# A hybrid encoder step on one core: sample caches read in turned order, new keys and rows written unturned, sample keys in blocks of 96, 96 and 80

## The chip, the core and the metric

The kernel runs on one core of one Trainium2 chip. The metric is the device time of one execution in microseconds (us); the figure given is the median of several runs. The profile is of one execution, taken by the hardware profiler. Engines are TensorE (PE; its weight loads are PEld), VectorE (DVE), ScalarE (ACT), GpSimd (POOL) and SyncE (SP). L12 is line 12 of the kernel before.

## What is computed

One layer of a streaming encoder, in float32, for 2048 prompt tokens (16 tiles of 128) and for a sample group of 8 streams with 16 new tokens each (one more tile of 128). Model width is 1024. What matters here of the reference:

```python
proj = h @ w_in                                   # q | k | v | u_val | u_gate, 512 each
k_ext = jnp.concatenate([past_k, k], axis=1)      # per stream 256 cached keys, 16 new ones
att = band_attention(q, k_ext, v_ext, ...)        # 8 heads of 64
u = u_val * jax.nn.sigmoid(u_gate)
u_ext = jnp.concatenate([conv_buf, u], axis=1)    # 30 cached rows, then a causal conv of width 31
new_k, new_v, new_conv = k_ext[:, -keep:], v_ext[:, -keep:], u_ext[:, -30:]
x = x + rmsnorm(jnp.concatenate([att, c], -1) @ w_out, g_mix_post)
mk, mv = (rmsnorm(mem, g_mem) @ w).reshape(...)   # 256 memory tokens, prompt only
x = x + rmsnorm(memory_attention(rmsnorm(x), mk, mv, w_mq, w_mo), g_mem_post)   # 4 heads of 256
x = x + rmsnorm((silu(h @ w_gate) * (h @ w_up)) @ w_down, g_ffn_post)
```

Outputs are the two activations, the newest keys, values and convolution rows of both groups, and the memory keys and values of the prompt. For the sample group the 256 memory keys and values per stream come in as caches.

## The kernel before, in words

Every product is made with float32 operands split in two parts, `hi` and `lo`, the second being what the rounding of the first left over (`mm3`, L286: three matmuls for one product, at L288, L289, L290; `mm3h`, L292, the same in two halves of 512 columns, at L296). ScalarE writes `hi`, VectorE or GpSimd subtracts (`wload`, L274: load on the SyncE queue, L277; cast, L281; subtraction, L283). Small products of the sample group's attention are plain float32, which the trace shows as two TensorE instructions each.

A matmul contracts over partitions, so operands must stand with the contracted index on partitions. What arrives with tokens on partitions is turned by `nc.tensor.transpose`, a matmul against the identity (`ident`) into PSUM, and copied out by ScalarE.

The phases, in order:

- **Memory phase** (`phase_mem`, L371). For `w_mk`, then `w_mv`: eight blocks of 128 output columns. Each block loads a weight block, makes 24 matmuls, and VectorE copies the result, with columns on partitions, into `yf` (L428, three buffers); splits of it go to `yh` and `yl` for the products that follow. For the output, `transp` (L410) turns each block with two transposes (L413) and two copies (L415) into `ot`, which is stored as rows at the end (L437).
- **Projections** (`phase_proj`, L464). Three groups of six (the last: five) tiles. First `conv_halo` (L483) brings the 30 cached convolution rows of each stream into `us`: two loads, eight transposes (L489), eight scaled copies (L491). Per group come gate and value products, the values `vo`, and then keys and queries in `qk` (L697). For tiles of 12 and over, the last group, `qk` copies each key tile (L721), transposes it (L723) and gathers it in `ko` (L726), stored as rows (L730, L732). The new convolution rows are turned too (L684 to L696). `tick` and `pump` mix in the convolution, on VectorE and GpSimd, at a rate per step.
- **Attention** (`attention`, L768). 128 units of one head and one tile, written out as a pipeline: scores at unit i, transposes of the probabilities four units later (L891), values six later (L904). `sample(s)`, L791, is a generator that handles stream s beside head s; the loop takes one of its steps every second unit from the second head on. Its steps: loads of the cached keys `kc`, values `vc` and new values `vn`; two steps of four transposes (L805) each with a copy into `kt` (L806); GpSimd's copy of the 16 new keys into `kt` (L808); scores over 272 keys (L819) and softmax; three transposes of the probabilities (L828); the value products. These take the keys in blocks of 128, 128 and 16: for each of four column groups two products with 128 partitions (L837) and one with 16 (L838).
- **Output projection and the sample group's memory attention** (`mixout`, L1000; `cross_sample`, L1085). The prompt tiles' products (L296) are the main stream. `cross_sample` is a generator of which one step is taken for every two of the eight weight blocks of a tile: norm, query product, 16 half streams of keys, softmax, 16 half streams of values, output product. `keys` (L1177) loads two blocks of 128 memory tokens per stream, and for each half of the width makes eight transposes (L1186) with two casts (L1188) and two subtractions (L1189); `Ahead` makes it two jobs early. `vals` (L1226) needs no transpose: `load` (L1105), then `split` (L1098: cast L1101, subtraction L1102). Both use three load buffers `wf`.
- **Prompt memory attention, gate and up, down.** The change does not touch their arithmetic. `shift_caches` (L1388) copies the kept part of the key and value caches from DRAM to DRAM during gate and up.

Storage is laid out by hand: a `Region` gives each name a place, a size and a count of buffers in a few large arenas, and names of different phases share places. The order of instructions on each engine comes from the tile framework, which orders the program when it is built by a simulated timeline (L1725), with some priorities set by hand. On the chip every engine and the SyncE queue then works through its own list in that order.

Of the kernel before, what the change touches and what calls it, by code (L numbers as in the profile page):

```python
# [31 lines left out]
PAST = 256  # L32
EPS = 1e-6
# [105 lines left out]
class Build:  # L139
# [22 lines left out]
    def early(self, ctx):  # L162
# [10 lines left out]
                   .lay(sbF, 18, ("kxx", 0.5, 2), ("vo", 1, 3), ("ko", 2, 5))  # L173
# [5 lines left out]
                        ("ctmp", 3, 2), ("qh", 1.5, 2), ("ql", 1.5, 2), ("kx", 0.5, 2))  # L179
# [191 lines left out]
    def phase_mem(self):  # L371
# [4 lines left out]
                .lay(fa, 0, ("f2o", 8, 2), ("ot", 4, 2), ("ss", 0.03125, 6), ("rstd", 0.03125, 6))  # L376
# [26 lines left out]
        for which, wn, on in ((0, "w_mk", "new_mem_k_prompt"), (1, "w_mv", "new_mem_v_prompt")):  # L403
# [3 lines left out]
            ot = [self.t(pool, [P, D], F32, "ot", 2) for _ in range(2)]  # L407
            prev = None

            def transp(j, yf):  # L410
                pt = self.t(ps_tr, [P, 2, P], F32, "tr")
                for i in range(2):
                    nc.tensor.transpose(pt[:, i, :], yf[:, i * P:(i + 1) * P], self.ident[:, :])  # L413
                for i in range(2):
                    nc.scalar.copy(ot[i][:, j * P:(j + 1) * P], pt[:, i, :])  # L415

            for j in range(KC):
# [14 lines left out]
                if prev is not None:  # L432
                    transp(*prev)
                prev = (j, yf)
            transp(*prev)
            for i in range(2):
                nc.sync.dma_start(A[on][i * P:(i + 1) * P, :], ot[i][:, :])  # L437
# [26 lines left out]
    def phase_proj(self):  # L464
# [18 lines left out]
        def conv_halo():  # L483
            for i in range(2):
                cc = self.t(pool, [P, D], F32, "xt", 2)
                nc.sync.dma_start(cc[:120, :512], A["cache_conv"][i * 120:(i + 1) * 120, :])
                pt = self.t(ps_tr, [P, 4, P], F32, "tr")
                for j in range(4):
                    nc.tensor.transpose(pt[:, j, :120], cc[:120, j * P:(j + 1) * P], self.ident[:120, :120])  # L489
                for j in range(4):  # L490
                    nc.scalar.activation(us[:, j, 4 * i:4 * i + 4, :HALO],  # L491
                                         pt[:, j, :120].rearrange("p (s w) -> p s w", w=HALO), AF.Copy, scale=2.0)
# [101 lines left out]
        kos = {}  # L594
        nxt = [norm_sub(GROUPS[0][0]), norm_sub(GROUPS[0][1])]
        conv_halo()
        for gi, subs in enumerate(GROUPS):
# [52 lines left out]
            for cg in range(2):  # L650
                wv = [self.wload(A["w_v"][cg, kh]) for kh in range(2)]
                for hsub, sub in zip(hs, subs):
                    hh, hl, _, _ = hsub
                    for i, t in enumerate(sub):
# [7 lines left out]
                        if t >= 12:  # L662
                            vo = self.t(pool, [P, 256], F32, "vo")
                            nc.scalar.copy(vo[:, :], ps[:, :256])
                            if t == S_TILE:
                                nc.sync.dma_start(self.vsamp[:, cg * 256:(cg + 1) * 256], vo[:, :])
                                nc.sync.dma_start(
                                    A["new_att_v_sample"][:, PAST - DEC_S:, cg * 256:(cg + 1) * 256], vo[:, :])
# [12 lines left out]
            if last:  # L681
                pt = self.t(ps_tr, [P, 4, P], F32, "tr")
                for j in range(4):
                    nc.tensor.transpose(pt[:HALO, j, :], uts[j][:, L:L + HALO], self.ident[:, :])  # L684
                un = self.t(pool, [P, 4, P], F32, "xn", 2)
                nc.scalar.activation(un[:HALO], pt[:HALO, 0:4, :], AF.Copy, scale=0.5)
                nc.sync.dma_start(A["new_conv_prompt"], un[:HALO].rearrange("p a b -> p (a b)"))
                pt = self.t(ps_tr, [P, 4, P], F32, "tr")
                for j in range(4):
                    uc = self.t(pool, [P, P], F32, "kx" + x_, 2)  # L690
                    nc.gpsimd.tensor_copy(uc[:, :].rearrange("p (s w) -> p s w", w=DEC_S), us[:, j, :, HALO:])
                    nc.tensor.transpose(pt[:, j, :], uc[:, :], self.ident[:, :])
                un = self.t(pool, [P, 4, P], F32, "xn", 2)
                nc.scalar.activation(un[:, :, :], pt[:, 0:4, :], AF.Copy, scale=0.5)
                nc.sync.dma_start(A["new_conv_sample"][:, HALO - DEC_S:, :],
                                  un[:, :, :].rearrange("p a b -> p (a b)"))  # L696
            def qk(which, j, blk, x):  # L697
# [14 lines left out]
                else:  # L712
# [4 lines left out]
                    for i, t in enumerate(sub):  # L717
                        if t < 12:
                            continue
                        kx = self.t(pool, [P, P], F32, "kx" + x_, 2)  # L720
                        nc.scalar.copy(kx[:, :], ps[:, i * P:(i + 1) * P])  # L721
                        pt = self.t(ps_tr, [P, 4, P], F32, "tr")
                        nc.tensor.transpose(pt[:, 0, :], kx[:, :], self.ident[:, :])  # L723
                        if j == 0:
                            kos[t] = self.t(pool, [P, 512], F32, "ko")
                        nc.scalar.copy(kos[t][:, j * P:(j + 1) * P], pt[:, 0, :])  # L726
                        if j < 3:
                            continue
                        if t == S_TILE:
                            nc.sync.dma_start(A["new_att_k_sample"][:, PAST - DEC_S:, :], kos[t][:, :])  # L730
                        else:
                            nc.sync.dma_start(A["new_att_k_prompt"][(t - 12) * P:(t - 11) * P, :], kos[t][:, :])  # L732
# [32 lines left out]
        nc.sync.dma_start(A["new_conv_sample"][:, :HALO - DEC_S, :],  # L765
                          A["cache_conv"].rearrange("(s w) d -> s w d", w=HALO)[:, DEC_S:, :])

    def attention(self):  # L768
        nc, A = self.nc, self.A
        sbF, sbR, ps, fa, fb = self.sbF, self.sbR, self.ps, self.fa, self.fb  # L770
        pool = (Region().lay(sbF, 34.5, ("kc", 4, 2), ("kt", 4.25, 1), ("pp", 1.5, 1), ("vn", 2, 1))
                .at("z", 2.5, (fa, [25, 22.5, 15, 20, 17.5]), (fb, [0, 2.5, 5]))
                .lay(fb, 7.5, ("vc", 4, 2), ("nmx", 0.03125, 12), ("sm", 0.03125, 2))
# [17 lines left out]
        def sample(s):  # L791
            kc = self.t(pool, [P, 2, 512], F32, "kc", 2)
            nc.sync.dma_start(kc[:, :, :], A["cache_att_k"][s].rearrange("(b p) d -> p b d", p=P))
            vc = self.t(pool, [P, 2, 512], F32, "vc", 2)
            nc.sync.dma_start(vc[:, :, :], A["cache_att_v"][s].rearrange("(b p) d -> p b d", p=P))
            vn = self.t(pool, [DEC_S, 512], F32, "vn", 2)
            nc.sync.dma_start(vn[:, :], self.vsamp[s * DEC_S:(s + 1) * DEC_S, :])
            yield
            kt = self.t(pool, [P, 4, PAST + DEC_S], F32, "kt", 1)
            for c2 in range(0, 4, 2):  # L800
                pt = self.t(ps_t, [P, 2, 2, P], F32, "t")
                for c in range(2):
                    for b in range(2):
                        cc = slice((c2 + c) * P, (c2 + c + 1) * P)
                        nc.tensor.transpose(pt[:, c, b, :], kc[:, b, cc], self.ident[:, :])  # L805
                nc.scalar.copy(kt[:, c2:c2 + 2, :PAST].rearrange("p c (b k) -> p c b k", k=P), pt[:, :, :, :])  # L806
                yield
            nc.gpsimd.tensor_copy(kt[:, :, PAST:], self.ksamp[:, :, s * DEC_S:(s + 1) * DEC_S])  # L808
# [17 lines left out]
            for b in range(3):  # L826
                w = P if b < 2 else DEC_S
                nc.tensor.transpose(pt[:w, b, :], z[:, b * P:b * P + w], self.ident[:, :])  # L828
            pp = self.t(pool, [P, 3, P], F32, "pp", 1)
            nc.scalar.copy(pp[:, :2, :], pt[:, :2, :])  # L830
            nc.scalar.copy(pp[:DEC_S, 2, :], pt[:DEC_S, 2, :])
            yield
            po = self.t(ps_o, [P, 4, 32], F32, "o")
            for c in range(4):
                cc, hc = slice(c * P, (c + 1) * P), slice(c * 32, (c + 1) * 32)
                for b in range(2):
                    nc.tensor.matmul(po[:, c, :], vc[:, b, cc], pp[:, b, hc], start=b == 0, stop=False)  # L837
                nc.tensor.matmul(po[:, c, :], vn[:, cc], pp[:DEC_S, 2, hc], start=False, stop=True)  # L838
# [246 lines left out]
    def cross_sample(self, pool, ps_so, ps_p):  # L1085
# [89 lines left out]
        kcs = {}  # L1175

        def keys(s, half):  # L1177
            if half == 0:
                kcs[s] = [load(A["cache_mem_k"][s, b * P:(b + 1) * P, :]) for b in range(2)]
            kh = self.t(pool, [P, 4, NM], F32R, "kvh")  # L1180
            kl = self.t(pool, [P, 4, NM], F32R, "kvl")
            for b in range(2):
                bs = slice(b * P, (b + 1) * P)
                pt = self.t(ps_p, [P, 4, P], F32, "p")
                for k in range(4):
                    nc.tensor.transpose(pt[:, k, :], kcs[s][b][:, (4 * half + k) * P:(4 * half + k + 1) * P],  # L1186
                                        self.ident[:, :])
# [541 lines left out]
```

## Time and profile before

| what | value |
|---|---|
| time, median of 3 runs | 3008.1 us (3006.89 to 3008.73) |
| span of the profiled execution, first to last instruction | 3000.1 us |
| mean granted TensorE clock | 0.990 |
| mean DMA rate over the span | 167 GB/s |
| DMA issue of memory keys, 16 times | 512 KB each |

How to read it: the busy time of an engine is the time in which at least one of its instructions runs. TensorE's instructions overlap, so the sum of their durations is more than its busy time, and a busy TensorE need not be at its peak. A wait is put down to the instruction that released it. The time outside the span is the start and the end of the program; the profiled execution has no time of its own besides its span.

### The profile page before, as it was taken

The numbers are of one execution on the slowest core, as the hardware profiler recorded it, in microseconds if no ns is written. First come the engines' busy times: TensorE is split into PE (matmuls) and PEld (weight loads), VectorE is DVE, ScalarE is ACT, GpSimd is POOL, SyncE is SP. The second block draws the span as 40 slices with busy tenths as digits, with TensorE's granted clock in tenths as the row PEclk, the third lists the DMA queues.
The fourth block names the chain that finished last, engine by engine and source line by source line (L and its number), as shares of the span: only waits on it lengthen the run. The fifth ranks groups of instructions, "written<-read, shape, count | busy, mean of one in ns | idle before, by whom it ended". The sixth has DMA issues, their size and how long they took to land.

```text
span 3000.1 us, 46145 instructions
## 1 busy us (share of the span) xinstructions
PE 2949.2 (98%) x16940; PEld 2714.6 (90%) x16940; DVE 2134.6 (71%) x3090; ACT 1360.3 (45%) x2731; POOL 1416.7 (47%) x1338
## 2 busy tenths in 40 slices
PE   9999999999999999999999999999999999999998
PEld 9999999989997887887888999999999999888777
DVE  6687886968776466435358888888788998555666
ACT  5535455668883344323334333433344444433433
POOL 0267496721123244136357565446555775424413
PEclk9999999989999999999999999999999999999999
DMA  7645253664435456323246333544334336756664
GB/s 278 246 138 185 88 170 108 201 213 168 155 138 175 169 199 205 105 87 133 88 163 222 116 137 124 196 153 152 134 134 157 142 140 205 256 176 215 217 223 148
DMA packets 197552, 499.57 MB, mean 167 GB/s; under 512 B 19334, under 2 KB 84750, under 8 KB 188485
## 3 DMA queue, kind: packets, MB, share of 16 engines
q1 hardware_dynamic: 182397, 427.01, 41.9%
q0 software_dynamic: 14928, 69.61, 6.2%
q8 instruction: 133, 2.18, 0.3%
q14 instruction: 94, 0.77, 0.1%
HBM read 365.45 MB, written 141.81 MB: 169 GB/s over the span
## 4 chain that ended last, share of the span: by engine, by line
PE 38%; DMA 4%; issue 3%; DVE 3%; POOL 3%; ACT 0%; SPq 0%; DVEq 0%; POOLq 0%; ACTq 0%
PE psb L290 12%; PE psb L288 12%; PE psb L289 12%; DMA sbf<-in_w_down_dram 2%; POOL sbf L1569 1%; PE psb L296 1%; DMA sbf<-x 1%; PE psb L1424 1%; DMA sbf<-hn 0%; DVE sbr L1639 0%; DVE sbr L1447 0%; POOL sbf L346 0%; DVE sbr L1573 0%; DMA sbf<-in_w_gate_dram 0%; DVE sbx L1447 0%
## 5 line engine op out<-in xcount | busy, mean ns | idle before, releaser
L288 PE MATMUL psb<-sbr 128*128 128x384 f32 (+3 forms) x2808 | 941.7, 337 | 4.1 <-DVE sbx L676 1.6
L289 PE MATMUL psb<-sbr 128*128 128x384 f32 (+3 forms) x2356 | 804.6, 342 | 0.4 <-DVE sbr L338 0.3
L290 PE MATMUL psb<-sbr 128*128 128x512 f32 (+3 forms) x1848 | 633.1, 344 | 4.3 <-DVE sbr L1639 4.1
L288 PEld LDWEIGHTS psb<-sbr 128*128 128x128 f32 x2808 | 529.2, 189 | 34.6 <-ACT sbr L1638 2.8
L290 PE MATMUL psb<-sbr,sbx 128*128 128x384 f32 (+2 forms) x1484 | 475.8, 321 | 0.0
L289 PEld LDWEIGHTS psb<-sbr 128*128 128x128 f32 x2356 | 443.9, 188 | 27.1 <-DVE sbr L1427 0.7
L290 PEld LDWEIGHTS psb<-sbr 128*128 128x128 f32 x1848 | 347.9, 188 | 34.9 <-DVE sbr L1639 8.2
L296 PE MATMUL psb<-sbr 128*128 128x512 f32 x1200 | 295.3, 394 | 1.9 <-ACT sbr L1317 1.1
L1447 DVE TENSOR_TENSOR sbr<-sbf,sbr 128x512 fp32r<-128x512 f32 x258 | 262.7, 1021 | 38.8 <-ACT sbr L1446 37.9
L1446 ACT CAST sbr<-sbf 128x512 fp32r<-128x512 f32 x258 | 159.2, 620 | 277.4 <-PE psb L289 229.3
L290 PEld LDWEIGHTS psb<-sbr,sbx 128*128 128x128 f32 x1484 | 279.6, 189 | 0.2
L542 DVE SCALAR_TENSOR_TENSOR psb<-sbf,psb 128x768 f32<-128x768 f32 (+1 forms) x290 | 264.3, 911 | 6.1
L296 PEld LDWEIGHTS psb<-sbr 128*128 128x128 f32 x1200 | 222.2, 189 | 47.6 <-ACT sbr L1317 1.3
L1639 DVE TENSOR_TENSOR sbr<-sbf,sbr 128x384 fp32r<-128x384 f32 (+2 forms) x242 | 168.1, 717 | 99.2 <-ACT sbr L1638 98.0
L283 POOL TENSOR_TENSOR sbx<-sbf,sbr 128x1024 fp32r<-128x1024 f32 (+1 forms) x62 | 155.0, 2501 | 84.8 <-ACT sbr L281 81.0
L1638 ACT CAST sbr<-sbf 128x384 fp32r<-128x384 f32 (+2 forms) x242 | 112.4, 483 | 174.1 <-PE psb L289 149.8
L1569 POOL TENSOR_TENSOR sbf<-sbf 128x512 f32<-128x512 f32 x77 | 106.5, 1390 | 168.7 <-DMA sbf<-in_w_down_dram 167.1
L552 POOL TENSOR_TENSOR flexb<-flexb,flexb 128x128 f32<-128x128 f32 (+1 forms) x180 | 168.9, 939 | 25.4 <-ACT flexb L551 15.1
L288 PE MATMUL psb<-sbr,sbx 128*128 128x384 f32 (+1 forms) x524 | 170.6, 327 | 1.8 <-ACT sbx L1446 1.1
L1446 ACT CAST sbx<-sbf 128x512 fp32r<-128x512 f32 x153 | 94.7, 620 | 163.4 <-PE psb L289 143.4
L1447 DVE TENSOR_TENSOR sbx<-sbf,sbx 128x512 fp32r<-128x512 f32 x153 | 153.4, 1004 | 17.0 <-ACT sbx L1446 16.8
L1441 POOL TENSOR_TENSOR sbf<-sbf 128x512 f32<-128x512 f32 x66 | 97.5, 1477 | 107.2 <-DVE sbr L1447 50.7
(350 smaller groups left out, 6281.5 us busy)
## 6 DMA issues: line engine op xcount, KB each, us to landing
af<-flexb SPq DMA_DIRECT2D x33, 1344.0 KB, 5.8
sbf<-in_w_down_dram SPq DMA_DIRECT2D x154, 256.0 KB, 3.5
sbf<-in_w_gate_dram SPq DMA_DIRECT2D x66, 512.0 KB, 3.3
sbf<-in_w_up_dram SPq DMA_DIRECT2D x66, 512.0 KB, 3.5
sbf<-af SPq DMA_DIRECT2D x85, 384.0 KB, 4.3
sbf<-x SPq DMA_DIRECT2D x49, 512.0 KB, 3.8
sbf<-in_w_in_dram SPq DMA_DIRECT2D x48, 512.0 KB, 3.8
sbr<-ks POOLq DMA_DIRECT2D x16, 1024.0 KB, 8.6
```

The lines of the kernel that those rows point to most:

```text
L283: self.lo_engine.tensor_tensor(lo[:, c], wf[:, c], hi[:, c].bitcast(F32), ALU.subtract)
L288: nc.tensor.matmul(ps, lh, rh, start=start, stop=False, **kw)
L289: nc.tensor.matmul(ps, lh, rl, start=False, stop=False, **kw)
L290: nc.tensor.matmul(ps, ll, rh, start=False, stop=stop, **kw)
L296: nc.tensor.matmul(y[o], l, r[:, o * 512:(o + 1) * 512], start=start and x == 0, stop=stop and x == 2)
L542: nc.vector.scalar_tensor_tensor(acc if w < CW - 1 else o, src(w), cwt[:, j, w:w + 1], acc, ALU.mult, ALU.add)
L552: nc.gpsimd.tensor_tensor(o, o, v, ALU.add)
L1446: nc.scalar.copy(hs[j][:, :], src[j])
L1447: nc.vector.tensor_tensor(ls[j][:, :], src[j], hs[j][:, :].bitcast(F32), ALU.subtract)
L1569: nc.gpsimd.tensor_tensor(acc[:, :], acc[:, :], q[:, :], ALU.add if s > 0 else ALU.subtract)
L1638: nc.scalar.copy(ch[:, m], a[:, x, m])
L1639: nc.vector.tensor_tensor(cl[:, m], a[:, x, m], ch[:, m].bitcast(F32), ALU.subtract)
```

## The change

Several inputs and outputs change their order in DRAM, done by the host on the arrays before and after (not part of the device time): cached keys, memory keys and cached convolution rows come in with the contracted index first; new keys, new convolution rows and the prompt's memory keys and values go out with it first. The sample group's new and kept rows go out as separate arrays. With that:

- the memory phase stores each `yf` block as it is, eight stores of 128 KB per matrix, and `transp` and `ot` go;
- `conv_halo` becomes one load and one scaled copy;
- in the last group `qk` copies keys from PSUM into one `ko` buffer of 8 KB per partition, stored once per column block, and the new convolution rows are copied and stored without a transpose;
- `sample` loads keys straight into `kt`, which now has two buffers, in its first step, and GpSimd's copy of the new keys moves there; its next two steps are empty, and the scores come one step earlier than before;
- the 272 keys of a sample are taken in blocks of 96, 96 and 80, with cached and new values in one tile (`vc` or `vd`, four loads with the one of the new values, three before);
- `keys` becomes load and split.

```diff
-        for which, wn, on in ((0, "w_mk", "new_mem_k_prompt"), (1, "w_mv", "new_mem_v_prompt")):
+        for which, wn, on in ((0, "w_mk", "new_mem_k_promptT"), (1, "w_mv", "new_mem_v_promptT")):
...
-                if prev is not None:
-                    transp(*prev)
-                prev = (j, yf)
-            transp(*prev)
-            for i in range(2):
-                nc.sync.dma_start(A[on][i * P:(i + 1) * P, :], ot[i][:, :])
+                nc.sync.dma_start(A[on][j * P:(j + 1) * P, :], yf[:, :])
...
         def conv_halo():
...
+            cc = self.t(pool, [P, 4 * DEC_B, HALO], F32, "xt", 2)
+            nc.sync.dma_start(cc[:, :, :], A["cache_convT"])
+            nc.scalar.activation(us[:, :, :, :HALO].rearrange("p j s w -> p (j s) w"), cc[:, :, :], AF.Copy, scale=2.0)
...
+                un = self.t(pool, [P, 4, HALO], F32, "xn", 2)
                 for j in range(4):
+                    nc.scalar.activation(un[:, j, :], uts[j][:, L:L + HALO], AF.Copy, scale=0.5)
+                nc.sync.dma_start(A["new_conv_promptT"], un[:, :, :].rearrange("p a b -> p (a b)"))
...
+                    if last:
+                        nc.scalar.copy(ko[:, j, col - 12 * P:col - 12 * P + npc], ps[:, :npc])
+                        if x:
+                            nc.sync.dma_start(A["new_att_k_promptT"][:, j, :], ko[:, j, :])
+                        if x and j == 3:
+                            nc.sync.dma_start(A["new_att_k_sampleT"], self.ksamp[:, :, :])
...
         def sample(s):
...
+            kt = self.t(pool, [P, 4, PAST + DEC_S], F32, "kt")
+            nc.sync.dma_start(kt[:, :, :PAST], A["cache_att_kT"][s])
+            vc = self.t(pool, [KB, 3, 512], F32, "v" + "dc"[s % 2])
+            nc.sync.dma_start(vc[:, :2, :], A["cache_att_v"][s, :2 * KB, :].rearrange("(b p) d -> p b d", p=KB))
+            nc.sync.dma_start(vc[:KL - DEC_S, 2, :], A["cache_att_v"][s, 2 * KB:, :])
+            nc.sync.dma_start(vc[KL - DEC_S:KL, 2, :], self.vsamp[s * DEC_S:(s + 1) * DEC_S, :])
+            nc.gpsimd.tensor_copy(kt[:, :, PAST:], self.ksamp[:, :, s * DEC_S:(s + 1) * DEC_S])
             yield
...
-                for b in range(2):
-                    nc.tensor.matmul(po[:, c, :], vc[:, b, cc], pp[:, b, hc], start=b == 0, stop=False)
-                nc.tensor.matmul(po[:, c, :], vn[:, cc], pp[:DEC_S, 2, hc], start=False, stop=True)
+                for b, w in blocks:
+                    nc.tensor.matmul(po[:, c, :], vc[:w, b, cc], pp[:w, b, hc], start=b == 0, stop=b == 2)
...
         def keys(s, half):
-            if half == 0:
-                kcs[s] = [load(A["cache_mem_k"][s, b * P:(b + 1) * P, :]) for b in range(2)]
...
+            return split(load(A["cache_mem_kT"][s, half])[:, :])
```

More of the change, by code (lines that the diff above doesn't have):

```diff
@@ L32 @@
 PAST = 256
+KB = 96
+KL = PAST + DEC_S - 2 * KB
 EPS = 1e-6
@@ L791, in sample @@
         def sample(s):
[L792 to L797, printed above, removed]
-            yield
[L799 to L802, printed above, removed]
-                    for b in range(2):
[L804 to L808, printed above, removed]
+            kt = self.t(pool, [P, 4, PAST + DEC_S], F32, "kt")
[5 more added lines that the diff above has]
+            nc.gpsimd.tensor_copy(kt[:, :, PAST:], self.ksamp[:, :, s * DEC_S:(s + 1) * DEC_S])
+            yield
+            yield
             yield
@@ L825, in sample @@
             pt = self.t(ps_t, [P, 3, P], F32, "t")
[L826 to L831, printed above, removed]
+            blocks = [(b, KB if b < 2 else KL) for b in range(3)]
+            for b, w in blocks:
+                nc.tensor.transpose(pt[:w, b, :], z[:, b * KB:b * KB + w], self.ident[:, :])
+            pp = self.t(pool, [KB, 3, P], F32, "pp", 1)
+            nc.scalar.copy(pp[:, :2, :], pt[:KB, :2, :])
+            nc.scalar.copy(pp[:KL, 2, :], pt[:KL, 2, :])
             yield
@@ L1174, in cross_sample @@
         jobs = [(s, b) for s in range(DEC_B) for b in range(2)]
-        kcs = {}
         def keys(s, half):
-            if half == 0:
-                kcs[s] = [load(A["cache_mem_k"][s, b * P:(b + 1) * P, :]) for b in range(2)]
[L1180 to L1187, printed above, removed]
-                nc.scalar.copy(kh[:, :, bs], pt[:, :, :])
-                nc.vector.tensor_tensor(kl[:, :, bs], pt[:, :, :], kh[:, :, bs].bitcast(F32), ALU.subtract)
-            return kh, kl
+            return split(load(A["cache_mem_kT"][s, half])[:, :])
         ahead = Ahead([lambda j=j: keys(*j) for j in jobs])
@@ L1391, in shift_caches @@
         src = self.A["cache_att_" + name][s, DEC_S:, :]
-        dst = self.A[f"new_att_{name}_sample"][s, :keep, :]
-        order = [[512, keep], [PAST * 512, 2], [1, 512]]
-        self.nc.sync.dma_start(bass.AP(dst.tensor, dst.offset, order), bass.AP(src.tensor, src.offset, order))
+        dst = self.A[f"new_att_{name}_sample"][s]
+        to, of = ([[512, keep], [rows * 512, 2], [1, 512]] for rows in (keep, PAST))
+        self.nc.sync.dma_start(bass.AP(dst.tensor, dst.offset, to), bass.AP(src.tensor, src.offset, of))
     def gate_up(self, ctx):
```

120 lines of the change are left out of this document (50 added, 70 removed).

## The prediction

> **What bounds the kernel now.** I read the page first, for the share of each engine, then the waits of TensorE alone, then single stretches of its timeline.
>
> ```profile
> span 3000.1 us, 46145 instructions
> PE 2949.2 (98%) x16940; PEld 2714.6 (90%) x16940; DVE 2134.6 (71%) x3090; ACT 1360.3 (45%) x2731; POOL 1416.7 (47%) x1338
> ```
>
> TensorE is busy for 2949.2 of 3000.1 us; no other engine passes 71%. So TensorE is idle for 50.9 us in all. Who ends those idle times, the longest, one in between and the shortest of 24 rows of the view of waits (total, times, longest):
>
> ```profile
> engine line waited for: us in total, times, longest us
> PE psb L874 <- DVE flexb L786: 5.6, 6, 1.7
> ...
> PE psb L296 <- DVE flexb L1102: 0.8, 1, 0.8
> ...
> PE psb L296 <- DVE sbr L283: 0.2, 1, 0.2
> ```
>
> No wait is worth more than 5.6 us, and they are scattered over many lines. The bound is the stream of matmuls, so an instruction taken out of that stream is worth what it holds the stream up for, wherever TensorE isn't waiting anyway. What is to be found is that price, which is not the duration in the rows: matmuls overlap.
>
> ```profile
> start us, us, engine line op out<-in xcount [idle before <-releaser]
> 1001.83 0.93 PE L1186 MATMUL psb<-ident,sbf 128*128 128x128 f32 x7
> 1002.51 1.63 PE L296 MATMUL psb<-sbr 128*128 128x512 f32 x6
> ```
>
> Seven transposes of the memory keys last 0.93 us together. One alone lasts 0.273 us (next fence), so the six after the first end (0.93 - 0.273)/6 = 0.11 us apart. That is the price of a transpose.
>
> **The change part by part.** The transposes that go, and the value products of the sample attention, in the view that groups by line and form (busy us, mean ns), then the one line of the conv halo (its x8 and durations):
>
> ```profile
> line engine op names shapes xcount | busy us, mean ns | idle before us <-releasers
> L1186 PE MATMUL psb<-ident,sbf 128*128 128x128 f32 x128 | 18.5, 273 | 0.0
> L805 PE MATMUL psb<-ident,sbf 128*128 128x128 f32 x64 | 10.2, 284 | 0.3 <-DVE sbr L893 0.3
> L413 PE MATMUL psb<-ident,sbf 128*128 128x128 f32 x32 | 6.1, 272 | 0.0
> L723 PE MATMUL psb<-ident,sbf 128*128 128x128 f32 x20 | 5.0, 272 | 0.0
> L837 PE MATMUL psb<-sbf,flexb 128*128 128x32 f32 x128 | 20.1, 281 | 0.1
> L838 PE MATMUL psb<-sbf 16*128 16x32 f32 x64 | 13.5, 291 | 0.0
> ```
> ```profile
> L489 PE MATMUL psb<-ident,sbf x8: 264/266/322, 131.0 to 135.1; 120*128 120x120 f32 x8
> ```
>
> *Transposes.* 128 + 64 + 32 + 20 + 8 = 252, and eight more by the code, four at L684 and four at L692: 260, all gone, at 0.11 us: 28.6 us. Not all of it is on the path. The eight of sample 0 and about four of the last keys fall in or beside the stretch from 620 to 643 us, where TensorE waits anyway (16.41 us busy of 23, fence of windows below): 12 x 0.11 = 1.3 us are worth nothing. The 32 of the memory phase and the eight of the halo, 40 x 0.11 = 4.4 us, stand ahead of the second phase, whose first normalisations want x tiles while the memory phase still loads its weights (DMA share 0.78 over 0 to 130 us): between nothing and all of it may come back as a wait there. I give back half, 2.2 us. Left: 28.6 - 1.3 - 2.2 = 25.1 us.
>
> *Blocks of 96, 96, 80.* Before, each of the four column groups of a sample issues four L837 (128 rows) and two L838 (16 rows). One group of sample 3:
>
> ```profile
> 762.79 0.63 PE L837 MATMUL psb<-sbf,flexb 128*128 128x32 f32 x4
> 763.35 0.40 PE L838 MATMUL psb<-sbf 16*128 16x32 f32 x2
> 763.69 0.63 PE L837 MATMUL psb<-sbf,flexb 128*128 128x32 f32 x4
> ```
>
> From group to group it is 763.69 - 762.79 = 0.90 us for six matmuls. Inside the run of four the step is (0.63 - 0.28)/3 = 0.117 us, so six in one stream would take 0.70: the two changes between 128 and 16 rows cost 0.20 us per group, and 32 groups cost 6.4 us. After, there are still six matmuls per group, of 96, 96 and 80 rows. No row shows 96 or 80. The nearest is the 120-row transposes of L489: seven of their eight last 264 to 266 ns or little more, like the 128-row ones. So I take the whole 6.4, with zero as the other end (each new height might need its own change).
>
> [...]
>
> *Clock.* The granted clock by stretch (length, busy time and count of each engine, clock, DMA share, GB/s):
>
> ```profile
> core 0: us, PE busy (x) PEld busy (x) DVE busy (x) ACT busy (x) POOL busy (x), PEclk, DMA share, GB/s
> 0.00:130.00 130.00, 127.67 (x880) 118.75 (x880) 89.91 (x139) 67.23 (x118) 22.18 (x33) 1.00 0.78 280
> 620.00:643.00 23.00, 16.41 (x64) 13.43 (x62) 15.65 (x36) 14.97 (x39) 6.59 (x14) 0.57 0.36 117
> 657.30:664.10 6.80, 6.80 (x30) 6.61 (x30) 3.37 (x9) 2.06 (x5) 0.94 (x2) 0.50 0.23 82
> 732.40:735.80 3.40, 3.40 (x17) 3.30 (x16) 2.76 (x7) 2.68 (x6) 0.29 (x2) 0.50 1.03 361
> 766.50:769.90 3.40, 3.40 (x16) 3.30 (x15) 3.11 (x7) 2.05 (x4) 0.05 (x1) 0.50 0.54 193
> 797.20:800.60 3.40, 3.40 (x14) 2.90 (x14) 0.45 (x3) 0.59 (x1) 0.29 (x2) 0.50 1.05 398
> 831.40:834.80 3.40, 3.40 (x18) 3.40 (x17) 2.21 (x6) 2.99 (x7) 0.29 (x2) 0.50 1.02 397
> 865.50:868.90 3.40, 3.40 (x17) 3.11 (x15) 2.27 (x6) 1.86 (x4) 0.00 (x0) 0.50 0.85 293
> ```
>
> In attention there are six half-clock stretches, 23.8 us, though TensorE is busy all through them: about 11.9 us of lost matmul time. The fourth row from below (766.5 us) begins just after the value block of sample 3, whose groups begin at 762.0 and step by 0.90, so end near 765.6. The block is a run of 24 matmuls of only 32 columns. After, it is 24 x 0.117 = 2.8 us long in place of 3.6, and has no drains, so a window of 3.4 us holds less thin work. Whether that keeps the clock up no row shows; I take half, 6.0 us, between zero and 11.9.
>
> [...]
>
> *ScalarE, VectorE, GpSimd.* The copies out of PSUM go with their transposes. In their place stand fourteen ScalarE copies at the projections (50 before), and 16 splits of memory keys of 1024 columns (32 of 512 before). I cost them at nothing: they lie behind the matmul stream on engines at 45 to 71%; without that cover a key split would cost its 2.3 us (1.05 + 1.22, rows at the last rival) per block. GpSimd's copy of the 16 new keys moves ahead to a sample's first step. Behind it in that queue stand the head loads, the memsets and the next normalisation; but it waits only for a reader two samples back, since `kt` now has two buffers.
>
> *Transfers.* The 16 loads of memory keys stay 16 of 512 KB. The value loads of the memory attention already run as the new key loads will, load, split, product:
>
> ```profile
> L1107 SPq DMA_DIRECT2D sbf<-in_cache_mem_k_dram x16: 327/328/422, 966.2 to 1060.5; - x16
> L1107 SPq DMA_DIRECT2D sbf<-in_cache_mem_v_dram x16: 327/328/333, 1061.8 to 1132.4; - x16
> ```
>
> Keys come every 94.3/15 = 6.3 us, values every 70.6/15 = 4.7 us, from the same buffers, and TensorE's wait on that split (L1102) is 0.8 us once. So keys can come at the pace of values. A sample's attention has four loads for three, issued three steps ahead of the scores. The memory phase stores 16 times 128 KB straight from `yf` where it stored four times 512 KB. VectorE's copy into `yf` must now wait for the landing of the store three blocks back:
>
> ```profile
> out_dram<-sbf SPq DMA_DIRECT2D x10, 128.0 KB, 2.4
> ```
>
> A store of this size lands in 2.4 us and three blocks take 9 (3.1 each, last rival): no cost, unless the queue itself stands, which is that rival.
>
> *Sum.* 25.1 + 6.4 + 6.0 = 37.5 us off a span of 3000.1: 2962.6. The profiled span lies 8.0 us below the median of 3008.1; the program's start and end lie outside it and stay. **Forecast: 3008.1 - 37.5 = 2970.6 us.** Its own ends: everything on the path and every clock fall gone, 28.6 + 6.4 + 11.9 = 46.9, 2961.2; only transposes and 4.4 given back, 28.6 - 1.3 - 4.4 = 22.9, 2985.2. Besides, the order on each engine is made anew at compile time, so the 50.9 us of idle time will fall differently; I allow a fifth of it, 10 us, either way.
>
> **The rivals.**
>
> *The clock falls as before:* thin work is not what brings it down, or 2.8 us of it is still enough. 37.5 - 6.0 = 31.5 us, 2976.6. For it: my half rests on no row of after. Against: five of the six falls come at a step of about 31 to 34 us, one per head, as the value blocks do. Chance 0.10. [...]
>
> *96 and 80 rows each drain as well,* and the clock falls as before: 31.5 - 6.4 = 25.1 us, 2983.0. For it: neither height is shown. Against: L489. Chance 0.08.
>
> *A load takes the place of the key transposes.* A key block now goes from landing through one whole cast and one subtraction before its matmuls, and if each of 16 blocks made TensorE wait for what its eight transposes took, 16 x 0.88 = 14.1 us come back: 37.5 - 14.1 = 23.4, 2984.7. Against: the value loads above. Chance 0.10.
>
> *Slower: the stores of the memory phase hold up its weights.* The SyncE queue works in order. A store of `yf` waits there for VectorE's copy, and weight loads placed behind it wait with it. Load, cast and subtraction of one block, and the eight copies of the first matrix:
>
> ```profile
> L277 SPq DMA_DIRECT2D sbf<-in_w_mk_dram x8: 327/328/536, 2.0 to 22.0; - x8
> DMA to landing us min/median/max: 4.9/5.5/6.2
> 63.62 1.05 ACT L281 CAST sbr<-sbf 128x1024 fp32r<-128x1024 f32 x1 [1.75 <-DMA sbf<-in_w_mv_dram]
> 61.90 1.22 DVE L283 TENSOR_TENSOR sbx<-sbf,sbr 128x1024 fp32r<-128x1024 f32 x1
> L428 DVE COPY sbf<-psb x8: 416/418/427, 16.3 to 37.7; 128x256 f32<-128x256 f32 x8
> ```
>
> A block needs 5.5 + 1.05 + 1.22 = 7.8 us from issue to use, and TensorE takes (37.7 - 16.3)/7 = 3.1 us per block. If each store stood right ahead of the very next block's load, TensorE would wait 7.8 - 3.1 = 4.7 us, 16 times: 75 us, 3008.1 - 37.5 + 75 = 3046. It decides from 37.5/16 = 2.3 us per block. With one more load ahead the wait is 7.8 - 6.2 = 1.6, and the kernel is still faster. Against: loads run several blocks ahead, the eighth is issued at 22.0 us, 15.7 us before the last copy at 37.7. Chance 0.05.
>
> *No difference:* some mixture of these that comes to nothing, 0.03. That the change doesn't do what it says can't be: the transposes have left the program.
>
> **How the numbers follow.** Forecast 0.64, then 0.10, 0.08, 0.10, 0.05, 0.03. About 0.2%, 6 us, is what a measurement of this kernel can tell from no change. The first four cases are faster: 0.92; same 0.03; slower 0.05. The range goes from the forecast's lower end less the 10 us, 2951, to the two rivals near 2984 with some of it, 2990.
>
> **What would show it.** The new trace should have some 260 fewer TensorE instructions, none at the transposes' lines; value blocks of 2.8 us without steps of 0.2; fewer half-clock stretches between 650 and 870 us; key loads every 5 us or less; TensorE idle 40 to 60 us in all. The prediction is wrong if TensorE's idle time grows by more than the sum, in the memory phase (weights late behind stores) or in the key stage (split late), or if the value blocks still take 0.9 us per group.

## The result, and the profile after

The changed kernel takes 2963.3 us (four executions, 2961.9 to 2963.8), the kernel before on the same chip 3007.5 us (3006.8 to 3008.7). The two medians differ by 44.2 us, a ratio of 0.9853. The estimate that the text goes by is a ratio of 0.9862, with a 95% interval of 0.9843 to 0.9880 that holds the other too: 41.5 us less, between 36 and 47. The forecast was 37.5 us less.

The page of the changed kernel, then the first and the last of its waits of TensorE (30 rows):

```profile
span 2960.8 us, 45532 instructions
PE 2905.3 (98%) x16680; PEld 2670.8 (90%) x16680; DVE 2131.0 (72%) x3074; ACT 1338.0 (45%) x2631; POOL 1418.2 (48%) x1334
```
```profile
engine line waited for: us in total, times, longest us
PE psb L830 <- DVE flexb L751: 5.5, 10, 1.7
...
PE psb L298 <- DVE sbr L1261: 0.2, 1, 0.2
```

TensorE has 16940 - 16680 = 260 instructions fewer, is busy 43.9 us less, and idle for 2960.8 - 2905.3 = 55.5 us in place of 50.9. It is still the bound, at the same 98%, and the longest row of waits is no longer than before (5.5 against 5.6 us).

One execution gave both the span of 2960.8 us and a time of 2962.9, so 2 us lie outside the span, not the 8.0 that the prediction took for it. In the experiments below 55 more executions of the kernel before took 2990.0 to 3011.5 us on other chips. So the profiled execution of before, at 3000.1 + 2 = 3002 us, was some 5 us quicker than the four that were timed, and the two traces differ by 39.3 us where the medians differ by 44.2. The experiments give their difference to the kernel before on their own chip, in us of its median there, about 3001 to 3003.

The value block of sample 3 in the changed kernel's timeline, where L794 is now all six products of a group:

```profile
739.78 0.53 PE L794 MATMUL psb<-sbf 96*128 96x32 f32 x4
740.14 0.63 PE L847 MATMUL psb<-ident,flexb 128*128 128x128 f32 x4
740.61 2.32 PE L794 MATMUL psb<-sbf 80*128 80x32 f32 x20
```

The run of twenty goes through both heights (the row names one form). Its step is (2.32 - 0.28)/19 = 0.107 us, so six instructions take 0.64 us where they took 0.90. There is no step of 0.2 at a change from 96 to 80 rows.

The prediction had not reckoned with the second row: four transposes of the head's probabilities stand between the first products and the rest. In this trace six of the eight value blocks are broken by other instructions in this way, in the trace of before none.

The granted clock (after the length: busy time and count of each engine, clock, DMA share, GB/s):

```profile
core 0: us, PE busy (x) PEld busy (x) DVE busy (x) ACT busy (x) POOL busy (x), PEclk, DMA share, GB/s
628.60:635.40 6.80, 5.12 (x16) 3.76 (x14) 4.39 (x9) 5.17 (x13) 3.15 (x6) 0.50 0.66 217
649.10:652.50 3.40, 3.40 (x17) 3.40 (x17) 1.99 (x7) 1.45 (x4) 0.89 (x2) 0.50 0.60 163
679.80:683.20 3.40, 3.40 (x16) 3.30 (x16) 1.70 (x5) 0.59 (x1) 0.00 (x0) 0.50 0.48 139
683.20:915.30 232.10, 225.79 (x1530) 206.32 (x1528) 184.47 (x427) 178.51 (x402) 42.11 (x56) 1.00 0.49 169
```

Around the value blocks of samples 0 and 1 the clock still falls; then it stays up for 232 us. Before, it fell around six of the eight. The first row is not at a value block: it is the turn to attention, where TensorE waits. There the half-clock time fell as well, from 2 x (1 - 0.57) x 23 = 19.8 us (the prediction's row of 620 to 643 us) to 6.8.

### The profile page after: what moved, and what is told of

It is laid out like the page before. It is cut to its first block, busy times and chain, and to the rows that moved or that the text cites. A ratio compares the mean times of both kernels' runs of the same rounds, so it can differ in the third digit from the quotient of the medians.

```text
span 2960.8 us, 45532 instructions
## 1 busy us (share of the span) xinstructions
PE 2905.3 (98%) x16680; PEld 2670.8 (90%) x16680; DVE 2131.0 (72%) x3074; ACT 1338.0 (45%) x2631; POOL 1418.2 (48%) x1334
## 4 chain that ended last, share of the span: by engine, by line
PE 40%; DVE 3%; DMA 3%; POOL 3%; issue 2%; ACT 1%; SPq 0%; DVEq 0%; POOLq 0%; ACTq 0%
PE psb L292 13%; PE psb L290 13%; PE psb L291 13%; DMA sbf<-in_w_down_dram 1%; PE psb L298 1%; POOL sbf L1512 1%; DMA sbf<-x 1%; DVE sbr L1582 1%; PE psb L1367 1%; DVE sbr L1390 0%; POOL sbf L348 0%; DVE sbx L1390 0%; DMA sbf<-hn 0%; DVE sbf L365 0%; DMA hn<-sbf 0%
```

## The experiments

Theory: every removed TensorE instruction is worth its step in the stream, a change of height 0.1 us (what the prediction and the texts below call a drain; what TensorE does in it no run shows), a half-clock stretch half its length, and the stretches come from concentrated thin work (the value blocks, whose products have only 32 columns). Rivals: a load takes the place of the transposes; stores hold up the memory phase; the transposes, not the value blocks, bring the clock down.

Each execution also reports its mean granted clock. One minus it, times two, times the span, is its half-clock time; in the table it is the mean over all executions of a kernel. The clock is given to 0.001, which is 6 us of half-clock time, so small differences in the last column mean little.

| kernel | ratio to before (95%) | us | half-clock us (mean clock) |
|---|---|---|---|
| before, 23 + 17 + 15 executions | 1 | 0 | 53 to 56 (0.9911, 0.9906, 0.9910) |
| changed | 0.9862 (0.9843 to 0.9880) | -41.5 | 34 (0.9942) |
| `d_attk`: cached keys of the sample attention | 0.9989 (0.9977 to 1.0001) | -3.3 | 64 (0.9893) |
| `d_blocks_b`: blocks 96, 96, 80 | 0.9958 (0.9945 to 0.9972) | -12.6 | 47 (0.9922) |
| `d_memk`: memory keys | 0.9955 (0.9939 to 0.9971) | -13.5 | 58 (0.9903) |
| `d_mem`: memory phase | 1.0000 (0.9991 to 1.0010) | 0.0 | 53 (0.9911) |
| `d_rows`: convolution rows and new keys | 0.9967 (0.9955 to 0.9980) | -9.9 | 47 (0.9922) |
| `d_order`: two height changes per sample | 0.9979 (0.9967 to 0.9991) | -6.3 | 49 (0.9918) |
| `d_split`: value products in two steps | 1.0014 (1.0004 to 1.0024) | +4.2 | 40 (0.9933) |
| `u_blocks`: changed, blocks put back | 0.9919 (0.9902 to 0.9935) | -24.3 | 55 (0.9908) |
| `u_mem`: changed, memory phase put back | 0.9870 (0.9853 to 0.9888) | -39.0 | 43 (0.9928) |
| `u_nostore`: changed, no stores there | 0.9862 (0.9847 to 0.9877) | -41.4 | 36 (0.9940) |
| `v_split`: changed, value products in two steps | 0.9850 (0.9837 to 0.9864) | -45.0 | 35 (0.9940) |

The table also holds a test of the price of half-clock time that needs no edit. The 55 executions of the kernel before are one program. A straight line through their times against their half-clock times, with one slope for the three chips, gives 0.46 us of time for each us at half clock (95% 0.36 to 0.56). So "worth half" holds here.

The five parts done alone add up to -3.3 - 12.6 - 13.5 + 0.0 - 9.9 = -39.3 us, against -41.5 for the whole. Their half-clock times do not add up so: +10, -7, +4, -3 and -7 us make -3, where the whole kernel has 20 less. The agreement of the two sums of time is in part luck.

How much the clock changes merely because a kernel was built anew can be read from three kernels in which the instructions of attention are the same as before, `d_rows`, `d_mem` and `d_memk`: 47, 53 and 58 us. Differences of 5 to 10 us in that column are therefore not by themselves the work of an edit.

**Cached keys alone.**

```diff
+            kt = self.t(pool, [P, 4, PAST + DEC_S], F32, "kt")
+            nc.sync.dma_start(kt[:, :, :PAST], A["cache_att_kT"][s])
...
-                        nc.tensor.transpose(pt[:, c, b, :], kc[:, b, cc], self.ident[:, :])
```

> The kernel before with the cached keys of the sample attention read in turned order alone; blocks stay 128, 128, 16. Theory (a transpose is worth 0.11 us of the matmul stream): 64 transposes go, 7.0 us, less 0.9 for sample 0: about -6 us against before; the half-clock stretches beside the value blocks stay, since the drains between 128 and 16 rows stay. [...]

Measured -3.3 us (-6.9 to +0.3). The half-clock time rose from 53 to 64 us. Taking 64 transposes out of the stream did not keep the clock up; it fell more often. The stretch from 643 to 870 us in the traces, before, then this kernel:

```profile
643.00:870.00 227.00, 226.19 (x1516) 212.17 (x1517) 175.59 (x426) 179.91 (x417) 28.76 (x52) 0.95 0.50 181
```
```profile
643.00:870.00 227.00, 223.94 (x1443) 209.68 (x1443) 171.80 (x412) 171.10 (x396) 27.95 (x50) 0.92 0.49 177
```

The mean clock is 0.92 in place of 0.95. That falsifies the rival by which the transposes bring the clock down. The sum, -6.1 for transposes and half of 11 us back, gives -0.6, inside the interval and near its upper end. With 64 transposes gone no gain of clock is seen here. That their going costs clock is not shown either: `u_blocks`, below, lacks them too and has 55 us, as before.

**Blocks alone.** First with a single buffer of cached keys, to make room:

```diff
-        pool = (Region().lay(sbF, 34.5, ("kc", 4, 2), ("kt", 4.25, 1), ("pp", 1.5, 1), ("vn", 2, 1))
+        pool = (Region().lay(sbF, 34.5, ("kc", 4, 1), ("kt", 4.25, 1), ("pp", 1.5, 1))
...
+                for b, w in blocks:
+                    nc.tensor.matmul(po[:, c, :], vc[:w, b, cc], pp[:w, b, hc], start=b == 0, stop=b == 2)
```

> The kernel before with the blocks of 96, 96, 80 alone (transposes of the cached keys stay; the buffer of cached keys is single to make room). Theory: 32 groups lose 0.20 us of drains, -6.4 us, and the shorter value blocks let the clock stay up in most samples, -6 to -12 us more: about -12 to -18 us, with two or fewer half-clock stretches between 700 and 870 us. Rival (96 and 80 rows drain as 16 did): groups keep 0.90 us, 0 us. Rival (the transposes bring the clock down): -6 us, five stretches stay.

Measured -12.0 us (-17.1 to -7.2). The sample group's attention comes out changed in this kernel, so its time is read only beside the repeat, which keeps the storage of before:

```diff
+            vc = self.t(pool, [KB, 2, 512], F32, "vc", 2)
+            nc.sync.dma_start(vc[:, :, :], A["cache_att_v"][s, :2 * KB, :].rearrange("(b p) d -> p b d", p=KB))
+            vn = self.t(pool, [KL, 512], F32, "vn", 2)
+            nc.sync.dma_start(vn[:KL - DEC_S, :], A["cache_att_v"][s, 2 * KB:, :])
```

> Again the kernel before with blocks of 96, 96, 80 alone, now with the storage of before (two buffers of cached keys; 192 value rows in one tile, 64 cached and 16 new ones in another), so that nothing but the blocks differs. Theory (drains 6.4 us, and shorter thin blocks keep the clock up): -10 to -15 us, groups of 0.70 us, three or fewer half-clock stretches between 700 and 870 us. Rival (the single key buffer was part of the earlier 12 us): -6 us.

Measured -12.6 us (-16.5 to -8.4). Two neighbouring groups of sample 2, and the clock over 643 to 870 us:

```profile
726.91 0.61 PE L840 MATMUL psb<-sbf,flexb 96*128 96x32 f32 x4
727.58 0.61 PE L840 MATMUL psb<-sbf,flexb 96*128 96x32 f32 x4
```
```profile
643.00:870.00 227.00, 225.76 (x1570) 213.65 (x1568) 181.21 (x438) 186.75 (x431) 31.71 (x54) 0.95 0.52 181
```

A group takes 0.67 us, 0.23 less than before, 7.4 us over 32 groups; the rival with no gain is out. The half-clock time fell by 7 us, worth 3.5. Together that is 10.9, inside the interval. But this trace does not show that the shorter blocks keep the clock up: at about 2.6 us each and in one piece, five of the eight have a half-clock stretch beside them, against six of before, and the mean clock of the stretch is the same 0.95. `d_rows`, which does not touch these blocks, also has 7 us less.

**Order of the value products.** The same 24 instructions per sample, the 16-row ones last:

```diff
+            for c in range(4):
+                cc, hc = slice(c * P, (c + 1) * P), slice(c * 32, (c + 1) * 32)
+                nc.tensor.matmul(po[:, c, :], vn[:, cc], pp[:DEC_S, 2, hc], start=False, stop=c == 3,
```

> The kernel before with one change of order: in each sample's value products all sixteen 128-row instructions come first, then all eight 16-row ones, so that the height changes twice per sample and not eight times. Theory (each change of height is a drain of about 0.1 us): 6 of 8 changes go, 8 x 6 x 0.1 = about -5 us, and the block is 3.0 us long in place of 3.6; if the clock follows the length of thin work, some half-clock stretches go too, to -10 us. Rival (16-row products are slow by themselves): 0 us.

Measured -6.3 us (-9.9 to -2.7). A block in its timeline:

```profile
758.10 1.86 PE L837 MATMUL psb<-sbf,flexb 128*128 128x32 f32 x16
759.90 1.07 PE L841 MATMUL psb<-sbf 16*128 16x32 f32 x8
760.90 0.66 PE L895 MATMUL psb<-ident,flexb 128*128 128x128 f32 x4
```

The block lasts 760.90 - 758.10 = 2.8 us, where before it went from 762.00 to 765.48, 3.5 us. Eight 16-row instructions in a row step by (1.07 - 0.29)/7 = 0.11 us: they are not slow by themselves; the change of height is. In this one trace the clock over 643 to 870 us is 0.98; over all executions the half-clock time is 49 us in place of 53, which a new build alone can do:

```profile
643.00:870.00 227.00, 226.02 (x1597) 213.40 (x1596) 183.43 (x444) 191.10 (x441) 33.47 (x54) 0.98 0.52 187
```

**Value products in two steps.** All height changes stay; two groups per step, in the kernel before and in the changed one:

```diff
+            for c0 in range(0, 4, 2):
+                po = self.t(ps_o, [P, 2, 32], F32, "o")
...
+                if c0 == 0:
+                    yield
```

> The kernel before with each sample's value products split over two steps, two column groups in each; all drains stay, and GpSimd's copy of the new keys joins the step before it. A thin block is 1.8 us long in place of 3.6, twice as often. Theory (the clock falls where a window of 3.4 us holds about 2.5 us or more of thin work): hardly any half-clock stretch between 650 and 870 us, about -6 to -10 us with the same drains. Rival (the drains or the amount of thin work bring it down, however spread): as before, 0 us.

Half of this came out as expected. Over 643 to 870 us the clock is 0.99, and over all executions the half-clock time is 40 us in place of 54, with every height change still there. So how the thin work is spread matters to the clock. Of the theory's two lengths, 3.4 us is that of the shortest half-clock stretches in the trace of before; the 2.5 us was a guess; no run measures a limit, and `d_blocks_b` falls about as often with blocks of 2.6 us as the kernel before with 3.5:

```profile
643.00:870.00 227.00, 222.92 (x1525) 203.79 (x1524) 179.99 (x444) 182.85 (x421) 28.69 (x52) 0.99 0.50 182
```

But the kernel is 4.2 us slower (1.2 to 7.2). Its waits between 868 and 905 us, where before has none:

```profile
engine line waited for: us in total, times, longest us
PE psb L840 <- DVE sbf L914: 4.0, 1, 4.0
PE psb L878 <- DVE flexb L786: 0.8, 2, 0.6
```

The second half of a sample shares one place in PSUM with the values of the head, and at the last sample waits 4.0 us for VectorE to empty it. TensorE is also idle for 227 - 222.92 = 4.1 us of the stretch above, before for 0.8. These waits, 8 us or so, and the half of 14 us of half-clock time nearly cancel. But over the whole trace TensorE is idle for 3002.7 - 2947.7 = 55.0 us against 50.9, only 4.1 more. What makes the kernel slower by 4 stays open.

> The changed kernel with the value products split over two steps, 1.4 us of thin work in each. Theory: the last half-clock stretches beside value blocks go (two in the changed kernel's trace, 6.8 us, so 3.4 us of work): about -45 us against before, 2 to 4 less than the changed kernel. Rival (the extra step and two more copies per sample cost VectorE as much): the changed kernel's time, -41 us.

Measured 2957.6 us, -45.0 (-48.9 to -40.8), lower than the changed kernel by 3.5, which the intervals do not tell apart (0.9837 to 0.9864 against 0.9843 to 0.9880). The half-clock time is 35 us against 34, so the gain that was expected of the clock does not show.

**Blocks put back in the changed kernel.**

```diff
-            vc = self.t(pool, [KB, 3, 512], F32, "v" + "dc"[s % 2])
+            vc = self.t(pool, [P, 2, 512], F32, "vc", 2)
+            vn = self.t(pool, [DEC_S, 512], F32, "vn", 2)
```

> The changed kernel with the blocks of 128, 128 and 16 put back, in a kernel without the transposes of the cached keys. Theory: drains come back, +6.4 us, and the half-clock stretches of the value blocks with them, +6 to +9: about -29 to -32 us against before. Rival (the clock follows the transposes): only the drains, -38 us.

Measured -24.3 us (-29.4 to -19.5), so the blocks are worth 17 us in the changed kernel, and 12.6 alone; the intervals do not tell the two apart. The half-clock time goes from 34 to 55 us, worth 10.5; with 6.4 that is 16.9. (`u_nostore`, with the new blocks and on the chip of `u_blocks`, has 36.) The same stretch in the changed kernel, then here:

```profile
643.00:870.00 227.00, 223.07 (x1582) 209.48 (x1581) 187.56 (x452) 189.14 (x436) 32.96 (x52) 0.98 0.51 178
```
```profile
643.00:870.00 227.00, 223.56 (x1467) 207.09 (x1465) 176.91 (x425) 175.61 (x405) 30.87 (x51) 0.94 0.50 178
```

These two kernels differ in nothing but the blocks and their storage. So in the changed kernel the blocks do keep the clock up, which they hardly did in the kernel before. Why the two surroundings differ is not shown. That other instructions break up most blocks of the changed kernel is not enough, for they do so here too.

**Memory keys alone.**

```diff
+            return split(load(A["cache_mem_kT"][s, half])[:, :])
```

> The kernel before with the memory keys read in turned order alone. Theory: 128 transposes at 0.11 us, -14 us. Rival (a load, cast and subtraction takes the place of the transposes): TensorE waits for splits in the key stage, 0 to -5 us. What the trace of the changed kernel shows from the last value product of attention to the last product of the output projection is 10 us less than before, between the two.

Measured -13.5 us (-18.3 to -8.7), the whole price of 128 transposes. The loads of the changed kernel:

```profile
L1063 SPq DMA_DIRECT2D sbf<-in_cache_mem_kT_dram x16: 327/328/333, 941.2 to 1017.2; - x16
L1063 SPq DMA_DIRECT2D sbf<-in_cache_mem_v_dram x16: 327/328/333, 1019.0 to 1092.8; - x16
```

Keys now come every 76.0/15 = 5.1 us, values every 4.9; the prediction had named 5 or less as a sign. In this stage of `d_memk` (960 to 1080 us) and of the changed kernel (920 to 1040 us) the view of waits has no row for TensorE. The rival is out.

**Memory phase.**

```diff
-            for i in range(2):
-                nc.sync.dma_start(A[on][i * P:(i + 1) * P, :], ot[i][:, :])
+                nc.sync.dma_start(A[on][j * P:(j + 1) * P, :], yf[:, :])
```

> The kernel before with the prompt's memory keys and values stored unturned alone (32 transposes and 32 copies go, sixteen stores of 128 KB come for four of 512 KB). Theory of the prediction: 3.5 us of TensorE's stream go, of which half may come back as a wait at the start of the projections: -1.7 to -3.5 us. Rival (weights come late behind the stores): 0 or slower, with TensorE waiting for casts and subtractions of weights between 20 and 110 us.

Measured 0.0 us (-2.7 to +3.0). TensorE's waits from 14 to 135 us:

```profile
engine line waited for: us in total, times, longest us
PE psb L288 <- ACT flexb L609: 1.4, 1, 1.4
PE psb L288 <- DVE flexb L433: 0.7, 1, 0.7
PE psb L288 <- ACT sbr L281: 0.3, 1, 0.3
PE psb L288 <- ACT sbr L337: 0.2, 1, 0.2
```

L609 is the first gate of the projections. Before, the same stretch has only the row of 0.2 us: so 2.4 of the 3.5 us come back around the turn to the second phase. Only 0.3 us of it is a wait for a weight's cast (L281). In the changed kernel the waits of this stretch are 0.8 us, with none at the gate, though between 10 and 110 us its queue waits 13 times at these stores (L424) for VectorE's copy (L420), 11.1 us in all. The kernel with the memory phase put back, and the one without its stores:

> The changed kernel with the memory phase put back (transposes, gathered rows, four stores). Theory: 1.7 to 3.5 us slower than the changed kernel, -41 to -42.5 us against before. Rival: the same time as the changed kernel or less, -44 us or more.

> The changed kernel without the sixteen stores of the memory phase; it leaves out two outputs, the prompt's memory keys and values. If the stores cost nothing, as the prediction has it: the changed kernel's time, -44 us against before, within 2. Rival (stores hold up the queue or the buffers): faster by what they cost, 3 us or more, and the excess of the memory phase goes.

`u_mem` measured -39.0 us (-44.1 to -33.6), `u_nostore` -41.4 (-45.9 to -36.9), the changed kernel -41.5. Whether the memory phase is worth 2.5 us in the changed kernel the intervals do not tell. That the stores cost no more than about 7 us they do, and the rival had reckoned with 75.

**Convolution rows and new keys alone.**

```diff
-                        nc.tensor.transpose(pt[:, 0, :], kx[:, :], self.ident[:, :])
...
+                        nc.scalar.copy(ko[:, j, col - 12 * P:col - 12 * P + npc], ps[:, :npc])
```

> The kernel before with the convolution rows and the new keys read and stored unturned alone: 8 + 8 + 20 transposes go. Theory: 36 x 0.11 = 4.0 us, less what comes back as a wait at the start of the projections and at the turn to attention, where TensorE waits anyway: -2 to -4 us. Rival (all of it lies where TensorE waits): 0 us.

Measured -9.9 us (-13.5 to -6.0), a miss: more than all 36 transposes are worth. Of it 7 us of half-clock time account for 3.5, though no instruction of the attention differs; 4.0 and 3.5 make 7.5, inside the interval. The clock in attention, 0.97 against 0.95:

```profile
643.00:870.00 227.00, 226.07 (x1555) 212.74 (x1554) 179.31 (x434) 183.37 (x425) 33.42 (x54) 0.97 0.49 173
```

Why the clock stays up better after this part is open. The order of all engines is made anew when the kernel is built, and with it the times at which the value blocks come; whether that is the cause no run shows.

## Why the prediction was right

- *The bound.* Right: TensorE at 98% before and after, and its idle time grew by 4.6 us, less than the 10 allowed.
- *0.11 us per transpose.* Right where it can be seen alone: 14.1 for the memory keys against 13.5 measured. 272 ns, their duration in the rows, would have given 35.
- *Half of the memory phase and halo given back.* Not decided. The halo was not run alone. Alone, the memory phase measured 0.0 us (-2.7 to +3.0), which holds both half and nothing, and 2.4 us came back in the place named, the start of the projections. In the changed kernel that wait is not there, and putting the phase back costs 2.5 us, within the intervals.
- *6.4 us for the height changes.* Right, and a little low: 0.64 us per group where 0.70 was forecast makes 0.26 x 32 = 8.3 us, and `d_order` shows the cause. The rival that 96 and 80 rows drain is out: the step is 0.107 us through both heights. (The row of L489 on which the forecast leaned gives only the shortest, median and longest of eight; that seven are alike it does not show.)
- *6.0 us for the clock.* The direction was right, the size too small, and the reason given held only in part. The term took half of the six stretches beside the value blocks; in the changed kernel two are left, and 20 us less half-clock time over its executions are worth about 9. `u_blocks` shows that the blocks are behind it there. But shorter blocks alone hardly lifted the clock in attention (`d_blocks_b`, 0.95), and in the traces 13 us of the gain lie at the turn to attention, which the sum did not consider. That the term came out near its size is partly luck.
- *The rival with the clock as before* is out (34 us against 55 with the old blocks). Idle time of TensorE does not explain the falls in attention: it was busy for all 23.8 us of the six stretches of before, and over 643 to 870 us the clock was 0.99 in `d_split` with 4.1 us idle, 0.95 before with 0.8.
- *A load in place of the transposes, and stores that hold up the queue.* Both out, by `d_memk` and `u_nostore`.
- *The 8.0 us outside the span.* Wrong: 2. The rest is that the profiled execution was quicker than the timed ones; the forecast did not hang on it, since it was a difference taken off the median.

By terms the changed kernel is now: about 25 us of transposes, 6.4 to 8.3 of height changes, about 9 of clock, 40 to 42 together, against 41.5 measured. That it meets it so closely is luck within an interval of 11 us.

## What to carry to other kernels

Where one engine is busy for 98% of the span, price a removed instruction by its step in the stream, end to end with its neighbours, not by its duration (0.11 us against 0.27 for a transpose here), and check whether it stands at a turn between phases, where it may be worth nothing (`d_mem`: 0.0 us for 32 transposes). Small products should not alternate between 128 and 16 rows (0.20 us per group of six here); blocks of 96, 96 and 80 rows avoid that and cost nothing that shows (0.107 us per instruction). Beside small products with few columns that stood together in one block the clock fell here (to 0.50, beside six blocks of eight); spreading them kept it up (half-clock time 40 us in place of 54, `d_split`), and yet did not make the kernel clearly faster (+4.2 us there, -3.5 within the intervals in `v_split`). Read the mean clock of many executions, not of one, before a few us are put down to anything else, and build a kernel that leaves the stage in question alone to see how far the clock moves by itself.

## What the runs showed of the hardware

- Two changes between 128 and 16 rows cost 0.20 us per group of six in the trace of before, about 0.1 us each; between 96 and 80 rows none shows (0.107 us per instruction throughout, in the trace of the changed kernel).
- The clock fell to 0.50 beside blocks of 24 gapless matmuls of 32 columns, though TensorE was not idle: beside six of eight in the trace of before. With the blocks in two parts of half the length it hardly did (`d_split`: mean clock 0.99 against 0.95 over the same 227 us; half-clock time 40 against 54 us over all executions). The length of the block alone did not decide it: 0.95 at 2.6 us (`d_blocks_b`), 0.98 at 2.8 (`d_order`).
- One us at half clock cost 0.46 us of time (0.36 to 0.56), from 55 executions of one program. A kernel with more clock was not always faster: `d_split` had 14 us less half-clock time and was 4.2 us slower.
- Executions of one and the same kernel spread over 21 us (2990.0 to 3011.5) on three chips, 10 to 17 us on each.
